# One core, a decoder layer with a 16,384-expert FFN: gathered tokens in groups of 32, finished in steps, and gate tables built by two engines

## The chip, the cores and the metric

The kernel runs on one core of a Trainium2 chip. The core has TensorE (PE, its weight loads shown as PEld), VectorE (DVE), ScalarE (ACT), GpSimd (POOL) and SyncE (SP), whose queue issues most transfers; GpSimd's own queue issues the indirect ones. The metric is the device time of one execution in microseconds, the median of several runs. All arithmetic is float32; large products are taken as three matmuls of a rounded part and a rest (hi and lo).

## The reference, cut to what matters

The layer mixes tokens (RWKV-7 and Mamba-2 heads), and then runs a PEER expert FFN over 512 tokens of width 2048. Only the last part is touched:

```python
def one_block(xb):
    q = (xb @ w_query).reshape(PEER_BLOCK, PEER_HEADS, 2, PEER_HALF)
    s = jnp.einsum('lhpd,hpnd->lhpn', q, sub_keys)
    s_half, i_half = lax.top_k(s, PEER_TOPK)
    ...                                   # 8 heads x 16 experts for each token
    eidx = jnp.take_along_axis(cand_i, pos, axis=-1)
    gates = jax.nn.softmax(top_s, axis=-1)
    u = u_emb[eidx]
    act = gelu(jnp.einsum('ld,lhkd->lhk', xb, u))
    return jnp.einsum('lhk,lhkd->ld', gates * act, v_emb[eidx])
h = h + gate2 * peer_ffn(n, ...)
return rms_norm(h, final_norm_w)
```

Each token so uses 128 of the 16,384 rows of u and of v.

## The kernel before

The FFN treats its tokens in two ways. The first 320 (TD) go **densely** through all experts; the last 192 (TG) have their 128 rows **gathered**.

Dense work comes in units, 128 of each kind. A u unit (`expert_u`) multiplies 128 experts' u rows with 320 tokens: 48 matmuls of 128x320 into `mm`, then a Gelu. Its weights come as four tiles `wr` of 256 KB; ScalarE casts each to `whi`, GpSimd subtracts for `wlo` (line 198). A v unit (`expert_v`) does the same with v rows (`vr`, `vhi`, `vlo`) into four tiles `po` that are added to the stream `hT`. Ahead of each four v units, `expert_g` takes a slice `gd` of the gate table, multiplies the activations by it and splits the product into `ghi` and `glo`.

The gate table says what weight each dense token gives each expert. `gate_block` builds it, ten blocks of 32 tokens: for each token two one-hot tiles of 128x128, J and I2 (I2 holds the gates), are made on VectorE by comparing with `iota`, and one matmul into `pg` multiplies them. ScalarE copies four tokens' result to `gb`, and a transfer of 2 MB writes the block to memory (`glD`), since v units read it in another order. The first v unit needs all ten blocks.

Gathered tokens are fed in between by `pace`, called once for each dense unit: it starts up to two gathers while the count of units allows it, spread over NGU of the 256 units, and at most NGB tiles `g` are held. A slot "u" gathers one row of u for each of 128 (token, slot) pairs, and VectorE takes the dot products with the tokens' rows, in two halves (line 1242). When a group is through, `weights` makes `wT`, the gates times the Gelu of the dot products. A slot "v" gathers one token's 128 rows of v; four tokens' gathers make four parts (`part`), each of which sums 512 columns of four tokens with four matmuls into four quarters of the tile `pw` (line 1258); ScalarE copies it, and a transfer writes `yG`. Parts are taken one at a time between the chunks of a dense unit.

When all slots are done, `gathered` reads `yG` back, turns it, adds it to the stream, takes the norm of all 192 tokens and writes them.

An engine works in the order of its instructions. That order is set by the Tile scheduler, which plays the program through; it is fixed when the kernel is built.

## Time and profile before

| | before |
|---|---|
| median of 3 runs | 4190.32 us (4183.4 to 4191.96) |
| profiled execution, its own time | 4183.04 us |
| its span | 4180.8 us |
| TensorE busy | 3789.5 us (91%) |
| VectorE busy | 2403.2 us (57%) |
| ScalarE busy | 1433.6 us (34%) |
| GpSimd busy | 2475.7 us (59%) |
| TensorE's mean granted clock | 0.941 |
| moved by transfers | 958.67 MB, mean 229 GB/s |

A busy share over the whole span is an average over stages with different limits; what bounds a stage is read from its own stretch. The granted clock is a share of full speed.

### The profile page before, as it was taken

How to read it: one execution, taken by the hardware profiler on the slowest of the kernel's cores; microseconds unless marked ns; L12 is line 12 of the kernel's file. 1: busy time of each engine (PE TensorE's matmuls, PEld its weight loads, DVE VectorE, ACT ScalarE, POOL GpSimd, SP SyncE). 2: the span in 40 equal slices, each digit the busy share in tenths (PEclk: the TensorE clock that was granted, in tenths of full speed). 3: DMA queues.
4: the chain of work that ended last, by engine and by line, in shares of the span. 5: the costliest groups of instructions: out<-in, count | busy, mean ns of one | idle time of the engine just before them, and what ended most of it. 6: DMA issues, size and time to landing. Idle time of an engine off the chain costs nothing. (4 is left out here: it accounts for less than half of the span.)

```text
span 4180.8 us, 65986 instructions
## 1 busy us (share of the span) xinstructions
PE 3789.5 (91%) x23694; PEld 3071.0 (73%) x23694; DVE 2403.2 (57%) x4909; ACT 1433.6 (34%) x2778; POOL 2475.7 (59%) x1919
## 2 busy tenths in 40 slices
PE   5899989999988996888688999999999999999978
PEld 3667656776657995777577877888787777777668
DVE  7442245466614999999867676667765221222234
ACT  3443324433324212222223333333333343433333
POOL 5445433433316434655377777888888776676646
PEclk9999999988969998998799999999999999999979
DMA  8465652333344225777688888897988788788843
GB/s 345 163 201 194 200 141 72 81 114 94 117 138 131 89 71 203 279 293 273 238 322 285 321 292 315 298 338 287 323 315 315 287 295 305 288 297 299 291 134 128
DMA packets 378503, 958.67 MB, mean 229 GB/s; under 512 B 62080, under 2 KB 127488, under 8 KB 322560
## 3 DMA queue, kind: packets, MB, share of 16 engines
q1 hardware_dynamic: 322880, 551.79, 40.1%
q0 software_dynamic: 55296, 402.68, 25.1%
q8 instruction: 186, 3.05, 0.3%
q14 instruction: 141, 1.16, 0.1%
HBM read 908.97 MB, written 45.29 MB: 228 GB/s over the span
## 5 line engine op out<-in xcount | busy, mean ns | idle before, releaser
L198 POOL TENSOR_TENSOR wlo<-wr,whi 128x512 fp32r<-128x512 f32 (+2 forms) x832 | 1119.3, 1357 | 939.0 <-ACT whi L197 829.0
L198 POOL TENSOR_TENSOR vlo<-vr,vhi 128x512 fp32r<-128x512 f32 x512 | 695.1, 1375 | 236.8 <-ACT vhi L197 213.4
L197 ACT CAST whi<-wr 128x512 fp32r<-128x512 f32 (+2 forms) x832 | 505.7, 616 | 908.8 <-PE mm L202 334.0
L203 PE MATMUL mm<-n2hi,wlo 128*128 128x320 f32 x2304 | 736.8, 320 | 27.6 <-POOL wlo L198 27.2
L201 PE MATMUL mm<-n2hi,whi 128*128 128x320 f32 x2304 | 735.3, 320 | 11.6 <-ACT whi L197 9.2
L202 PE MATMUL mm<-n2lo,whi 128*128 128x320 f32 x2304 | 726.3, 315 | 2.4 <-POOL n2lo L198 2.4
L201 PE MATMUL po<-ghi,vhi 128*128 128x320 f32 x2048 | 627.9, 316 | 38.9 <-DVE hT L1207 18.8
L202 PE MATMUL po<-glo,vhi 128*128 128x320 f32 x2048 | 628.6, 313 | 14.0 <-DVE glo L198 14.0
L1242 DVE SCALAR_TENSOR_TENSOR g<-g,row 128x1024 f32<-128x1024 f32 x384 | 616.5, 1645 | 5.4 <-DMA g<-in_u,eix 5.4
L203 PE MATMUL po<-ghi,vlo 128*128 128x320 f32 x2048 | 527.7, 318 | 25.2 <-POOL vlo L198 24.7
L197 ACT CAST vhi<-vr 128x512 fp32r<-128x512 f32 x512 | 311.8, 620 | 596.1 <-PE mm L202 308.0
L203 PEld LDWEIGHTS mm<-n2hi,wlo 128*128 128x128 f32 x2304 | 440.3, 191 | 99.4 <-issue 48.6
L1166 DVE TENSOR_TENSOR act<-gd,act 128x320 f32<-128x320 f32 x128 | 162.5, 1279 | 605.2 <-ACT act L1139 528.0
L201 PEld LDWEIGHTS mm<-n2hi,whi 128*128 128x128 f32 x2304 | 442.0, 192 | 38.5 <-issue 18.5
L202 PEld LDWEIGHTS mm<-n2lo,whi 128*128 128x128 f32 x2304 | 442.0, 192 | 25.1 <-issue 21.8
L201 PEld LDWEIGHTS po<-ghi,vhi 128*128 128x128 f32 x2048 | 389.0, 191 | 89.8 <-issue 28.1
L1207 DVE SCALAR_TENSOR_TENSOR hT<-po,mod,hT 128x320 f32<-128x320 f32 x512 | 248.5, 543 | 324.8 <-PE po L203 311.3
L203 PEld LDWEIGHTS po<-ghi,vlo 128*128 128x128 f32 x2048 | 356.6, 191 | 88.2 <-POOL vlo L198 42.3
L202 PEld LDWEIGHTS po<-glo,vhi 128*128 128x128 f32 x2048 | 390.9, 191 | 31.4 <-issue 15.9
L1258 PE MATMUL pw<-g,wT 128*32 128x512 f32 x1536 | 293.6, 617 | 20.2 <-ACT ys L1261 11.6
L1235 POOL DMA_INDIRECT g<-in_u,eix x192 | 227.7, 1186 | 120.5 <-DVE I L1127 29.2
L201 PE MATMUL mm<-nhi,whi 128*128 128x512 f32 x640 | 261.4, 408 | 4.5 <-ACT whi L197 4.5
(438 smaller groups left out, 5890.3 us busy)
## 6 DMA issues: line engine op xcount, KB each, us to landing
wr<-in_uT SPq DMA_DIRECT2D x512, 256.0 KB
vr<-in_v SPq DMA_DIRECT2D x512, 256.0 KB
wr<-in_wrest SPq DMA_DIRECT2D x160, 256.0 KB
aw<-in_ada SPq DMA_DIRECT2D x32, 1024.0 KB
a2w<-in_adar SPq DMA_DIRECT2D x64, 512.0 KB
glD<-gb SPq DMA_DIRECT2D x10, 2048.0 KB
gd<-glD SPq DMA_DIRECT2D x32, 640.0 KB
a3w<-in_adar SPq DMA_DIRECT2D x32, 512.0 KB
```

Of the source, the lines that this page charges most:

```text
L197: copied.append(S.copy(hi, src))
L198: return (eng or V).tensor_tensor(lo, src, hi.bitcast(F32), OP.subtract)
L201: TE.matmul(ps, lhsT=whi, rhs=xhi, start=first, stop=False)
L202: TE.matmul(ps, lhsT=whi, rhs=xlo, start=False, stop=False)
L203: done_mm[0] = TE.matmul(ps, lhsT=wlo, rhs=xhi, start=False, stop=last)
L1166: V.tensor_tensor(a.rearrange("p (b t) -> p b t", t=TB), gd[:, :, i, :], a.rearrange("p (b t) -> p b t", t=TB), OP.mult)
L1207: V.scalar_tensor_tensor(h, po[d], mod2[:, 48 + k:49 + k], h, OP.mult, OP.add)
L1235: G.indirect_dma_start(out=g, out_offset=None, in_=I[s[0]], in_offset=bass.IndirectOffsetOnAxis(ap=ix, axis=0))
L1242: V.scalar_tensor_tensor(g[:, c], g[:, c], 1.0, n2s[i][:, c], OP.mult, OP.mult, accum_out=wtp[i][:, e, n:n + 1])
L1258: TE.matmul(ps[32 * j:32 * j + 32, :], lhsT=wT[:, t0 + j:t0 + j + 1].to_broadcast([P, 32]), rhs=gs[j][:, cq], start=True, stop=True, tile_ ...
```

## The change

- **Groups.** Gathered tokens form six groups of 32, each token with four rows of partitions; a u slot gathers 32 tokens x 4 experts. Before, there was one group of 128 tokens and one of 64 with two rows each. Indices and gates take a way through memory (`exD`, `gaD`) to get into that shape. `wT` is made by VectorE's transpose of 32x32 blocks.
- **Order of the slots.** The u slots run 38 slots ahead; then u and v alternate. NGU is 222 (was 200), NGB 6 (was 7), NSP 36 (was 30): the number of u units before the first v unit.
- **v rows summed singly.** One token makes one part: four matmuls, one for each 512 columns of its one gather.
- **Finishing in steps.** After each 64 tokens, five steps (`end_steps`) run between dense units in place of `gathered`.
- **Gate tables.** J for four tokens is one TENSOR_TENSOR; of four I2, two are made by VectorE as before and two by two activations of ScalarE.

```diff
-NGU = 200
+NGU = 222
-NGB = 7
+NGB = 6
-NSP = 30
+NSP = 36
...
+    V.tensor_scalar_mul(ngT, gT[:, 0:TD], -1.0)
...
+            J = gx.tile([P, 4, P], F32, name="J", bufs=2)
+            V.tensor_tensor(J, iota.unsqueeze(1).to_broadcast([P, 4, P]),
+                            jT[:, t0:t0 + 4].unsqueeze(2).to_broadcast([P, 4, P]), OP.is_equal)
+            I2 = gx.tile([P, 4, P], F32, name="I2", bufs=2)
             for i in range(4):
-                J = gx.tile([P, P], F32, name="J", bufs=4)
-                I2 = gx.tile([P, P], F32, name="I2", bufs=4)
-                V.tensor_scalar(J, iota, jT[:, t:t + 1], None, OP.is_equal)
-                V.tensor_scalar(I2, iota, iT[:, t:t + 1], gT[:, t:t + 1], OP.is_equal, OP.mult)
+                if i % 2:
+                    V.tensor_scalar(I2[:, i], iota, iT[:, t:t + 1], gT[:, t:t + 1], OP.is_equal, OP.mult)
+                else:
+                    S.activation(I2[:, i], iota, AF.Abs, bias=iT[:, t:t + 1], scale=-1.0)
+                    S.activation(I2[:, i], I2[:, i], AF.Relu, bias=gT[:, t:t + 1], scale=ngT[:, t:t + 1])
...
-    slots = [("u", 1, n) for n in range(64)] + [("v", n) for n in range(4)]
-    for n in range(P):
-        slots += [("u", 0, n)] + [("v", 4 + n // 2)] * (n % 2 and n < 120)
-    slots += [("v", n) for n in range(64, TG)]
+    for n in range(TG + NS + 6):
+        slots += [("u", n // NS, n % NS)] * (n < TG) + [("v", n - NS - 6)] * (n >= NS + 6)
...
+            if late and late[0][0] <= units:
+                late.pop(0)[1]()
...
+                V.transpose(wT[:, 32 * i:32 * i + 32], wts)
...
-        four.append((g, i))
-        if len(four) < 4:
-            return
+        def part():
             ps = pw2.tile([P, T], F32, name="pw")
-            for j in range(4):
-                TE.matmul(ps[32 * j:32 * j + 32, :], lhsT=wT[:, t0 + j:t0 + j + 1].to_broadcast([P, 32]), rhs=gs[j][:, cq],
+            for q in range(4):
+                TE.matmul(ps[32 * q:32 * q + 32, :], lhsT=wT[:, i:i + 1].to_broadcast([P, 32]), rhs=g[:, T * q:T * q + T],
...
+            if i % TF == TF - 1:
+                late.extend((units + 2 + n, f) for n, f in enumerate(end_steps(i // TF)))
...
+        def add(e):
+            ps = pu.tile([P, 8, TF], F32, name="mm", tag="mm")
+            for d in range(8):
+                TE.transpose(ps[:, d, :], o[0:TF, P * k:P * k + P], ident[0:TF, 0:TF])
+            V.tensor_tensor(sq[:, ks], ps, colk(mod2[:, 48 + 8 * e:56 + 8 * e]), OP.mult)
+            V.tensor_tensor(hg[:, ks], hg[:, ks], sq[:, ks], OP.add)
+            S.activation(sq[:, ks], hg[:, ks], AF.Square)
+            V.tensor_tensor(hg[:, ks], hg[:, ks], colk(col("fw", 8 * e, 8)), OP.mult)
+        def norm():
+            V.tensor_reduce(acc, sq.rearrange("p k t -> p t k"), mybir.AxisListType.X, OP.add)
+            TE.matmul(ps[:, 0:TF], lhsT=ones, rhs=acc, start=True, stop=True)
+            G.tensor_tensor(rn, rn, negh[:, 0:1].to_broadcast([P, TF]), OP.pow)
+            V.tensor_tensor(hg[:, ks], hg[:, ks], rn.unsqueeze(1).to_broadcast([P, 8, TF]), OP.mult)
+            nc.sync.dma_start(out.rearrange("k p t -> p k t")[:, :, TD + TF * f:TD + TF * f + TF], hg)
...
+        return [load, lambda: None, lambda: add(0), lambda: add(1), norm]
```

How this stands in the engines' orders, at three places. First the gate stage. On VectorE, before, between two dot products (`g,wtp<-g,row`) of a u slot:

```order
L1242 SCALAR_TENSOR_TENSOR g,wtp_14866<-g,row 128x1024 x2
L1126 TENSOR_SCALAR J<-iota,jT 128x128
L1127 TENSOR_SCALAR I_15092<-iota,iT,gT 128x128
L1126 TENSOR_SCALAR J<-iota,jT 128x128
L1127 TENSOR_SCALAR I_15097<-iota,iT,gT 128x128
L1126 TENSOR_SCALAR J<-iota,jT 128x128
L1127 TENSOR_SCALAR I_15102<-iota,iT,gT 128x128
L1126 TENSOR_SCALAR J<-iota,jT 128x128
L1127 TENSOR_SCALAR I_15107<-iota,iT,gT 128x128
L1242 SCALAR_TENSOR_TENSOR g,wtp_14866<-g,row 128x1024 x2
```

and on VectorE after, in the same stage:

```order
L1254 SCALAR_TENSOR_TENSOR g,wtp<-g,row 128x1024 x2
L1130 TENSOR_TENSOR J<-iota,jT 128x512
L1136 TENSOR_SCALAR I_15177<-iota,iT,gT 128x128 x2
L1130 TENSOR_TENSOR J<-iota,jT 128x512
L1136 TENSOR_SCALAR I_15192<-iota,iT,gT 128x128 x2
L1254 SCALAR_TENSOR_TENSOR g,wtp<-g,row 128x1024 x2
```

Eight instructions for four tokens became three, and twice as many tokens stand between two u slots. On ScalarE after, where only casts, `gb` copies and Gelus stood, the activations of I2 stand among them:

```order
L1142 COPY gb<-pg 128x128x4
L1139 ACTIVATE I_15254<-iota,iT 128x128 x2
L199 CAST whi<-wr 128x512 x2
L1140 ACTIVATE I_15254<-I_15254,gT,ngT 128x128
L1139 ACTIVATE I_15269<-iota,iT 128x128 x2
L1140 ACTIVATE I_15254<-I_15254,gT,ngT 128x128
L199 CAST whi<-wr 128x512
L1140 ACTIVATE I_15269<-I_15269,gT,ngT 128x128 x2
L1152 ACTIVATE act<-mm 128x320
```

A cast of `whi` now stands behind activations that write a buffer which an earlier gate matmul reads.

Second, the parts on TensorE late in the program, before, with the dense matmuls (`po`) around them:

```order
L1258 MATMUL pw<-g,wT 32x512 x3
L201 MATMUL po<-ghi,vhi 128x320
L202 MATMUL po<-glo,vhi 128x320
...
L202 MATMUL po<-glo,vhi 128x320
L1258 MATMUL pw<-g,wT 32x512
L201 MATMUL po<-ghi,vhi 128x320
L202 MATMUL po<-glo,vhi 128x320
...
L1258 MATMUL pw<-g,wT 32x512 x4
```

and after:

```order
L205 MATMUL mm<-n2hi_11455,wlo 128x320
L1268 MATMUL pw<-g,wT 32x512 x4
L203 MATMUL mm<-n2hi_11456,whi 128x320
...
L205 MATMUL po<-ghi,vlo 128x320 x4
L1268 MATMUL pw<-g,wT 32x512 x4
L203 MATMUL po<-ghi,vhi 128x320
```

Before, a first part stands as three matmuls and, 24 dense matmuls on, one; in the whole order the 768 matmuls stand in 262 such pieces. After, they stand in 191, all but a few of them of four.

Third, GpSimd's queue at the first of the three finishing steps, after; `rnf` is the tile whose power is taken, `g` are gathers:

```order
L1247 DMA g<-in_u,eix 128x2048
L200 TENSOR_TENSOR vlo<-vr,vhi 128x512 x3
L1247 DMA g<-in_v,eT 128x2048
L1309 TENSOR_TENSOR rnf<-rnf,negh 128x64
L200 TENSOR_TENSOR wlo<-wr,whi 128x512 x4
L1247 DMA g<-in_u,eix 128x2048
```

The power over 64 columns stands between the splits of two dense units; before, one power over two columns stood in `gathered`.

## Rows read from the trace of the kernel before

**Rows 1.** Busy us and instructions of each engine in seven stretches

```profile
core 0: us, PE busy (x) PEld busy (x) DVE busy (x) ACT busy (x) POOL busy (x), PEclk, DMA share, GB/s
1624.70:2054.50 429.80, 324.97 (x1984) 304.94 (x1984) 408.21 (x875) 119.20 (x223) 231.98 (x172) 0.87 0.77 281
2054.50:2404.50 350.00, 311.52 (x1865) 272.27 (x1866) 246.33 (x335) 107.09 (x197) 257.78 (x199) 0.95 0.86 306
2404.50:3268.20 863.70, 809.64 (x5036) 695.13 (x5036) 582.19 (x674) 292.70 (x536) 722.29 (x536) 0.99 0.87 309
3268.20:3956.20 688.00, 684.51 (x4426) 536.07 (x4424) 169.49 (x221) 272.81 (x482) 482.34 (x408) 1.00 0.81 295
3956.20:4014.60 58.40, 27.30 (x97) 8.58 (x97) 12.02 (x35) 10.94 (x25) 4.87 (x5) 0.55 0.38 136
4014.60:4164.00 149.40, 149.24 (x1010) 148.97 (x1008) 56.73 (x93) 63.15 (x115) 103.61 (x80) 0.99 0.44 143
4164.00:4180.80 16.80, 1.73 (x9) 1.25 (x9) 8.01 (x19) 1.98 (x5) 4.17 (x5) 0.60 0.46 156
```

**Rows 2.** The same stretches, the part sums (tile pw) alone: PE, PEld, ACT

```profile
2054.50:2404.50 350.00, 31.92 (x138) 4.54 (x138) 9.55 (x17) 0.95 0.86 306
2404.50:3268.20 863.70, 96.02 (x427) 13.29 (x427) 31.84 (x55) 0.99 0.87 309
3268.20:3956.20 688.00, 151.50 (x919) 21.64 (x919) 66.82 (x114) 1.00 0.81 295
3956.20:4014.60 58.40, 14.74 (x58) 1.61 (x58) 4.68 (x8) 0.55 0.38 136
```

**Rows 3.** The gate stage, the gate matmuls (tile pg) alone: PE, PEld, ACT

```profile
1624.70:2054.50 429.80, 134.68 (x640) 110.48 (x640) 44.41 (x80) 0.87 0.77 281
```

**Rows 4.** Timeline of TensorE: start us, us, what; a part in pieces

```profile
3401.54 1.05 PE L1258 MATMUL pw<-g,wT 128*32 128x512 f32 x2
...
3406.23 1.06 PE L1258 MATMUL pw<-g,wT 128*32 128x512 f32 x8
```

**Rows 5.** Tiles J, I, oh and glo: ns min/median/max, first and last start

```profile
L1126 DVE TENSOR_SCALAR J<-iota,jT x320: 268/279/5569, 1622.6 to 2040.0; 128x128 f32<-128x128 f32 x160
...
L1127 DVE TENSOR_SCALAR I<-iota,iT,gT x320: 328/340/5610, 1622.9 to 2040.2; 128x128 f32<-128x128 f32 x160
...
L1075 DVE TENSOR_TENSOR oh<-pf,iota x8: 414/418/419, 1612.1 to 1617.2; 128x256 f32<-128x256 f32 x8
...
L198 DVE TENSOR_TENSOR glo<-act,ghi x4: 484/484/486, 2055.1 to 2056.3; 128x320 fp32r<-128x320 f32 x4
```

**Rows 6.** Groups by line on VectorE, 1680 to 2060: busy us, mean ns

```profile
L1127 DVE TENSOR_SCALAR I<-iota,iT,gT 128x128 f32<-128x128 f32 x288 | 145.6, 506 | 0.0
L1242 DVE SCALAR_TENSOR_TENSOR g<-g,row 128x1024 f32<-128x1024 f32 x104 | 136.1, 1343 | 0.0
L1126 DVE TENSOR_SCALAR J<-iota,jT 128x128 f32<-128x128 f32 x288 | 127.0, 441 | 3.8 <-PE pg L1128 3.7
L1242 DVE DVE_READ_ACCUMULATOR g<-g,row 128x1 f32 x104 | 8.4, 81 | 0.0
```

**Rows 7.** Groups by line, 2400 to 3200

```profile
L198 DVE TENSOR_TENSOR glo<-act,ghi 128x320 fp32r<-128x320 f32 x45 | 86.8, 1932 | 20.5 <-ACT ghi L197 19.6 <-issue 0.8
```

**Rows 8.** Tile row on ScalarE

```profile
L299 ACT COPY row<-mps x8: 265/266/277, 45.1 to 142.8; 128x128 f32<-128x128 f32 x8
```

**Rows 9.** Timeline at the end of the gate stage

```profile
1979.69 0.61 PE L1128 MATMUL pg<-I,J 128*128 128x128 f32 x4
...
2042.08 0.32 SPq L1130 DMA_DIRECT2D glD<-gb  x1
...
2053.45 1.70 DVE L1166 TENSOR_TENSOR act<-gd,act 128x320 f32<-128x320 f32 x4 [12.86 <-DMA gd<-glD]
```

**Rows 10.** Groups by line and shape on GpSimd: powers over eight and two columns

```profile
L597 POOL TENSOR_TENSOR rnb<-rnb,negh 128x8 f32<-128x8 f32 x8 | 13.1, 1640 | 10.7 <-DVE rnb L594 10.7
...
L938 POOL TENSOR_TENSOR rn<-rn,negh 128x2 f32<-128x2 f32 x1 | 0.7, 725 | 44.6 <-DVE rn L937 44.6
```

**Rows 11.** Stretches as in rows 1, from 3000 us

```profile
3000.00:3100.00 100.00, 94.58 (x588) 81.99 (x587) 76.41 (x87) 33.26 (x61) 87.70 (x64) 1.00 0.94 341
```

More of the change, by code (lines that the diff above doesn't have):

```diff
@@ L959, in _hybrid @@
     gT = gp.tile([P, T], F32, name="gT")
-    n2D = dp.tile([2, P, D], F32, name="n2D")
+    n2D = dp.tile([TG, D], F32, name="n2D")
     yG = dp.tile([TG, D], F32, name="yG")
-    ggt = [gq.tile([P, n], F32, name=f"ggt{n}") for n in (P, 64)]
-    eix = [gq.tile([P, n], U32, name=f"eix{n}") for n in (P, 64)]
+    exD = dp.tile([TG, P], U32, name="exD")
+    gaD = dp.tile([TG, P], F32, name="gaD")
+    ggt = gq.tile([P, TG // 32, NS], F32, name="ggt")
+    eix = gq.tile([P, TG // 32, NS], U32, name="eix")
     eT = gq.tile([P, TG], U32, name="eT")
@@ L1152, in _hybrid @@
     units = 0
-    done = []
+    late = []
+    ended = [0]
     def expert_g(grp):
-        gd = vp.tile([P, TD // TB, 4, TB], F32, name="gd", bufs=1)
+        gd = vp.tile([P, TD // TB, 4, TB], F32, name="gd", bufs=2)
         nc.sync.dma_start(gd, glD.rearrange("b j i t -> j b i t")[:, :, 4 * grp:4 * grp + 4, :])
@@ L1167, in expert_g @@
                             a.rearrange("p (b t) -> p b t", t=TB), OP.mult)
-            ghi = vp.tile([P, TD], F32R, name="ghi", bufs=5)
-            glo = vp.tile([P, TD], F32R, name="glo", bufs=5)
+            ghi = vp.tile([P, TD], F32R, name="ghi", bufs=8)
+            glo = vp.tile([P, TD], F32R, name="glo", bufs=8)
             split(ghi, glo, a, V)
@@ L1202, in expert_v @@
             if grp == 31:
-                sqs = vp.tile([P, 4, TD], F32, name="gd", bufs=1)
+                sqs = vp.tile([P, 4, TD], F32, name="gd", bufs=2)
             for d in range(4):
@@ L1213, in expert_v @@
             pace(last)
-            if not (slots or begun or parts or done):
-                done.append(True)
-                gathered()
             if nu < min(128, 4 * grp + 8):
@@ L1219, in expert_v @@
                 nu += 1
-    wts = [gq.tile([P, n], F32, name=f"wts{n}") for n in (P, 64)]
-    wtp = [gq.tile([P, 2, n], F32, name=f"wtp{n}") for n in (P, 64)]
+    wts = gq.tile([P, NS], F32, name="wts")
+    wtp = gq.tile([P, 2, NS], F32, name="wtp")
     begun = []
-    four = []
     held = [0]
@@ L1231, in gather @@
             n2s[s[1]] = va.tile([P, D], F32, name="row", bufs=1)
-            nc.sync.dma_start(n2s[s[1]], n2D[s[1]])
+            for q in range(4):
+                nc.sync.dma_start(n2s[s[1]][32 * q:32 * q + 32, :], n2D[32 * s[1]:32 * s[1] + 32, :])
         held[0] += 1
-        ix = eix[s[1]][:, s[2]:s[2] + 1] if s[0] == "u" else eT[:, s[1]:s[1] + 1]
+        ix = eix[:, s[1], s[2]:s[2] + 1] if s[0] == "u" else eT[:, s[1]:s[1] + 1]
         G.indirect_dma_start(out=g, out_offset=None, in_=I[s[0]], in_offset=bass.IndirectOffsetOnAxis(ap=ix, axis=0))
@@ L1254, in part @@
-        def part(q):
-            cq = slice(T * q, T * q + T)
+            if n == NS - 1:
+                V.tensor_tensor(wts, wtp[:, 0], wtp[:, 1], OP.add)
+                S.activation(wts, wts, AF.Gelu)
+                V.tensor_tensor(wts, wts, ggt[:, i, :], OP.mult)
+                V.transpose(wT[:, 32 * i:32 * i + 32], wts)
+            return
+        def part():
             ps = pw2.tile([P, T], F32, name="pw")
-            for j in range(4):
-                TE.matmul(ps[32 * j:32 * j + 32, :], lhsT=wT[:, t0 + j:t0 + j + 1].to_broadcast([P, 32]), rhs=gs[j][:, cq],
-                          start=True, stop=True, tile_position=(0, 32 * j))
-            ys = vp.tile([P, T], F32, name="ys", bufs=2)
+            for q in range(4):
+                TE.matmul(ps[32 * q:32 * q + 32, :], lhsT=wT[:, i:i + 1].to_broadcast([P, 32]), rhs=g[:, T * q:T * q + T],
+                          start=True, stop=True, tile_position=(0, 32 * q))
+            ys = gq.tile([P, T], F32, name="ys", bufs=2)
@@ L1261, in part @@
             S.copy(ys, ps)
-            for j in range(4):
-                nc.sync.dma_start(yG[t0 + j:t0 + j + 1, cq], ys[32 * j:32 * j + 1, :])
-            held[0] -= 4 * (q == 3)
-        parts.extend(lambda q=q: part(q) for q in range(4))
-    def weights(i):
-        w = wts[i]
-        V.tensor_tensor(w, wtp[i][:, 0], wtp[i][:, 1], OP.add)
-        S.activation(w, w, AF.Gelu)
-        V.tensor_tensor(w, w, ggt[i], OP.mult)
-        ps = pw2.tile([P, T], F32, name="pw")
-        if i == 0:
-            TE.transpose(ps[:, 0:P], w, ident)
-            S.copy(wT[:, 64:TG], ps[:, 0:P])
-        else:
-            for hs in (slice(0, 64), slice(64, 128)):
-                TE.matmul(ps[hs, 0:64], lhsT=w[hs, :], rhs=ident[hs, hs], start=True, stop=True)
-            S.copy(wT[:, 0:64], ps[:, 0:64])
@@ L1326, in _hybrid @@
         expert_v(grp)
-    while slots or begun or parts:
+    while slots or begun or parts or late:
         while parts:
@@ L1331, in _hybrid @@
         pace(done_mm[0])
-    if not done:
-        gathered()
     rr = rms_all(pu, "mm", gq, sacc[:, 0:TD])
-    rs = vp.tile([P, TD], F32, name="ghi", bufs=5)
+    rs = vp.tile([P, TD], F32, name="ghi", bufs=8)
     S.copy(rs, rr)
```

86 lines of the change are left out of this document (39 added, 47 removed).

## Prediction

> **What bounds the kernel now.** I read the stretches first, cutting the span where the work changes [rows 1]. The profiled execution took 4183.04 us: a span of 4180.8 and 2.2 around it; the median of the runs shown, 4190.32, is 7.3 above that, and I sum against the profiled execution. Nothing ahead of 1624.7 us stands in another order but for a few small copies, so the sum starts there.
>
> The first stretch (1624.7 to 2054.5) builds the gate tables beside the first dense units. The reader is to see VectorE busy for 408 of its 430 us while TensorE is busy for 325 at a granted clock of 0.87: VectorE bounds it. The four stretches behind it hold the rest of the 254 dense units. Take the part sums [rows 2] and the gate matmuls [rows 3] from TensorE's counts in [rows 1] and divide by 48: 28, 36, 96, 73 and 21 units. The last 21 have nothing beside them: 149.4/21 = 7.11 us each, which I take as TensorE's price of a dense unit. With it, 688 us of the fourth stretch leave 688 - 73 x 7.11 = 169 us for its parts, and TensorE is busy throughout: TensorE bounds it. The second and third stretch run with u and v tokens in flight; there something else costs 0.8 to 1.7 us a unit (below). Between them and the last 21 units lie 58.4 us in which TensorE does 27 us of work at half clock: the gathered tokens are finished in one piece, and TensorE, which works in program order, stands.
>
> **The parts.** A part is four matmuls into four column quarters of one tile. In the trace a stretch of one such matmul (two records) takes 1.05 us, and one of all four (eight records) 1.06 [rows 4]: the four run side by side, and one alone costs as much. Before, the four come from four gathers, and the first part of a batch often stands in pieces, as the order's rows show. Counting such pieces in the whole order gives 262 before and 191 after, when all four matmuls hang on one gather. Along the timeline the second stretch has 28 of the 262, the third 90, the fourth 143, and one run of 29 matmuls lies in the 58 us (58 records [rows 2]). So a piece costs 169/143 = 1.18 us in the fourth stretch, and the change takes 261 - 191 = 70 pieces off: 70 x 1.18 = 83 us, certain where TensorE bounds, less where it waits anyhow.
>
> **The gate stage.** J was four TENSOR_SCALAR per four tokens (median 279 ns), now one TENSOR_TENSOR over 512 columns. TENSOR_TENSOR takes 418 ns for 256 columns and 484 for 320 [rows 5], 1.03 ns a column, so 682 ns for 512, against 4 x 279 = 1116. Half of I2 stays on VectorE. In this stretch I2 took 506 ns and J 441 on average, half a dot product 1343 and its read 81 [rows 6]. After: 80 x 0.682 + 160 x 0.506 + some 49 u slots (38, and half of the rest of 62) x 2 x 1.42 = 55 + 81 + 140 = 276 us, against 408. The upper bound is VectorE held up by GpSimd: glo, a TENSOR_TENSOR of 320 columns, averages 1932 ns in the middle of the span [rows 7], which would make J 3.1 us and the sum 247 + 81 + 140 = 468.
>
> By the rows, then, J gets shorter by 0.43 us a group [rows 5]. A rule of the Trainium skill speaks against this edit: VectorE: DVE Perf Modes, section Why `tensor_tensor` can't do 2×_2P or 4×, says that tensor_tensor keeps to one element a cycle in float32 where tensor_scalar may take two. By that rate alone J's 512 columns would take twice as long as now; the rows hold the slower rate already and still come out shorter, since three of four fixed costs go.
>
> ScalarE gets 320 activations of 128 columns; the nearest row is 266 ns for a copy of that size [rows 8], 85 us in all, beside 119 us that it is busy there now: 204 of some 400 us. That is cover enough if nothing waits in its queue; a rival below is that it does.
>
> TensorE is then next: 34 units (the 28 and six more, by NSP 36 for 30) x 7.11 = 242; 320 gate matmuls between 98 us (four records, two matmuls, in 0.61 us [rows 9]) and 135 (their busy time now, waits among them [rows 3]); ten parts, 12 us. That is 352 to 389 us; with 0.8 us of waiting a unit up to 416. I take **400**, so v starts at 2025, not 2054, with six more units done. At the end of the stage before, the last table goes to memory, comes back and is multiplied: from 2042.1 to 2053.5 with TensorE idle [rows 9]. After, the order has the last gate matmul three units (some 25 us) ahead of the first v unit, which hides these 11 us.
>
> **The paced stretch.** 226 - 6 = 220 units remain: 220 x 7.11 = 1564, and 181 pieces x 1.18 = 214. Waits: the second stretch before has 350 - 36 x 7.11 - 28 x 1.18 = 61 us over (1.7 a unit), the third 864 - 96 x 7.11 - 90 x 1.18 = 75 (0.8 a unit). By the list of slots the third runs two u to one v, and 427/8 = 53 v tokens [rows 2] in 96 units make 0.55 v and 1.1 u a unit. After, 384/222 = 1.73 slots go with each unit, u and v in turn from the 39th on, 0.87 each: less VectorE work a unit than in the third, and GpSimd as busy: there it has 722/96 = 7.5 us a unit [rows 1], four splits and some 1.64 gathers, and here a tenth of a gather more. I take the third's 0.8 for the units with u tokens in flight, from the 36th to the 200th (the last u is slot 346, and 346/1.73 = 200): 164 x 0.8 = 131 us. Bounds: 0 (as in the fourth stretch) and 1.7 (as in the second), so 0 to 279.
>
> **The finishing.** The 58.4 us go. In their place come three times five steps between units. Sixteen transposes each lie on TensorE (48 in all, about 15 us with short waits for their tile). One step is dearer than it looks: GpSimd's pow now runs over 64 columns. Pow took 725 ns for 2 columns and 1640 for 8 [rows 10], 0.15 us a column, so about 10 us for 64. The rows of the order show what stands behind it in GpSimd's queue: four splits of wlo, for which TensorE waits. ScalarE and GpSimd run up to four tiles (one unit) ahead, which covers a part; I take 7 us each, 20 in all, between 0 and 30.
>
> An I2 of 340 ns took up to 5610 [rows 5], so VectorE is at times held for the length of GpSimd's work. The Trainium skill, SBUF — State Buffer, section Who interferes with whom, says that GpSimd and a VectorE operation with two SBUF inputs, or in a two-port mode, exclude each other for the whole instruction. By that rule VectorE would stand for the same 10 us, three times, and the sum would be up to 10 us more where TensorE then waits for glo.
>
> **Sum.** 1624.7 + 400 + 1564 + 214 + 131 + 20 + 15 + 16.8 (the last stretch, unchanged) = 3985.5, and 2.2 around it: **3988**, 195 us less than the profiled execution.
>
> **The rivals.**
> Transfers bind (chance 0.17). A unit moves four tiles of 256 KB and 1.73 gathers of 128 rows of 8 KB (1.049 MB), with the gate slices 2.94 MB. At 7.11 + 0.87 x 1.18 + 0.8 = 8.9 us that is 329 GB/s. The third stretch averaged 309 with queues 0.87 busy; for it speaks that over 300 is rare. Against it, one stretch of 100 us moved 341 at 0.94 [rows 11]. Held to 309, a unit takes 9.5 us: 0.6 x 164 + 0.4 x 26 = 108 us more, 4096.
> The waits nearly vanish (0.13), since u tokens are spread thinner: without 131 and 20 it is 3837; half of it, 3912.
> The tables move the work but don't shorten the stage (0.08), if J is held up as glo is: 468 + 27 us in place of 400, so 4083.
> ScalarE's queue stalls, and the kernel is slower (0.03). The activations of I2 stand ahead of casts of whi, for which splits and dense units wait, and an activation waits until TensorE has read the I2 of two groups ago, which hangs on J. If each of the 80 groups holds the queue for more than 195/80 = 2.4 us, all is lost; at 3 us it is 4228. Against it: in the order an activation has a cast or copy on either side, and ScalarE idles half of that stage.
> No change (0.01) would need the pieces, the stand of 58 us and the stage all to be covered by something unseen.
>
> **How the numbers follow.** The forecast has the remaining 0.58, 3930 to 4040 for its own part. From 3880 to 4100 the range takes in the forecast, the transfers' case, the held J and half of the case without waits; what is left out is the other half, the slower case and tails. About 0.2%, some 8 us, is what a measurement of this kernel can tell from no change. Faster by more: 0.95; within: 0.01; slower: 0.04.
>
> **What would show it.** Right: VectorE below 0.8 busy in the gate stage and v's first matmul near 2025; stretches of eight records wherever parts stand; no stand of TensorE near the end, and 26 units at 7.1 us; three pows of about 10 us. Wrong: a rate that stays at 309 GB/s with queues near 0.9 and units of 9.5 us; wlo as what ends most of TensorE's idle time; whi late by ScalarE in the gate stage.

## The result, and the profile after

The changed kernel took 4037.31 us (median of four runs, 4028.36 to 4060.61) beside 4191.14 for the kernel before on the same chip: a ratio of 0.9645, 95% interval 0.9603 to 0.9688. It is faster, by 154 us. The profiled execution took 4028.36 us, a span of 4026.3. The sum had given a span of 3985.5, so 41 us have to be explained. This execution was the fastest of the four; the median lies 9 us above it.

The page after, the line of busy times and the line of transfers. TensorE is busy 128 us less than before, and 6 MB more are moved:

```profile
PE 3661.0 (91%) x23705; PEld 3044.2 (76%) x23705; DVE 2398.0 (60%) x4504; ACT 1521.6 (38%) x3090; POOL 2547.7 (63%) x1921
...
DMA packets 392370, 964.60 MB, mean 240 GB/s; under 512 B 76080, under 2 KB 141360, under 8 KB 335920
```

The stretches after, cut again where the work changes; they answer to [rows 1]:

```profile
core 0: us, PE busy (x) PEld busy (x) DVE busy (x) ACT busy (x) POOL busy (x), PEclk, DMA share, GB/s
1617.00:2029.00 412.00, 349.07 (x2335) 323.69 (x2333) 329.77 (x443) 242.76 (x574) 277.85 (x198) 0.95 0.88 322
2029.00:2345.70 316.70, 286.50 (x1790) 247.84 (x1791) 218.38 (x305) 104.16 (x195) 243.58 (x184) 0.95 0.91 323
2345.70:2635.00 289.30, 271.85 (x1806) 237.79 (x1805) 189.56 (x215) 104.47 (x193) 252.16 (x189) 0.99 0.94 337
2635.00:2690.00 55.00, 45.67 (x300) 39.82 (x299) 40.86 (x41) 17.53 (x33) 46.66 (x30) 0.91 0.77 286
2690.00:3318.00 628.00, 581.01 (x3770) 506.93 (x3769) 391.11 (x453) 216.15 (x405) 515.49 (x394) 0.97 0.92 328
3318.00:3372.00 54.00, 43.90 (x286) 37.84 (x286) 37.60 (x41) 17.21 (x32) 44.78 (x29) 0.91 0.75 275
3372.00:3580.00 208.00, 192.78 (x1253) 168.28 (x1255) 131.11 (x149) 71.93 (x134) 176.38 (x133) 0.97 0.93 334
3580.00:3800.00 220.00, 220.00 (x1499) 181.15 (x1492) 47.38 (x75) 90.75 (x162) 160.94 (x134) 1.00 0.87 297
3800.00:3860.00 60.00, 53.22 (x352) 52.44 (x352) 23.93 (x31) 21.18 (x38) 46.79 (x29) 0.94 0.49 148
3860.00:4009.00 149.00, 149.00 (x1017) 148.76 (x1015) 49.87 (x80) 63.66 (x117) 106.30 (x83) 1.00 0.41 136
4009.00:4026.30 17.30, 1.76 (x10) 1.24 (x9) 8.20 (x19) 2.17 (x5) 4.18 (x5) 0.63 0.44 152
```

The reader is to see five things. The gate stage ends at 2029 and holds 34 units, counted from 1610.6, where the third dense unit begins (the sum counts from the same unit, 1624.7 in the kernel before). The stretch behind it (2029 to 2346) is 33 v units back to back: TensorE's counts divided by 48, as in the prediction, leave 316.7 - 33 x 7.11 - 26 x 1.18 = 51 us of waiting, 1.6 a unit. Of these TensorE is idle for 30; for the other 21 it is busy longer than its price, at a granted clock of 0.95. The other stretches up to 3580, without the finishings, have 0.9 a unit, with GpSimd busy for 0.82 to 0.87 of the time. The three finishings (55, 54 and 60 us) hold some 38 us more than their units. From 3580 to 4009 TensorE is busy without a gap but for the third finishing, and no stand is left at the end.

One part of the gain is luck. The first Gelu of a dense unit, in the profile before and in the one after:

```profile
L1139 ACT ACTIVATE act<-mm x128: 427/432/444, 1624.2 to 4136.1; 128x320 f32<-128x320 f32 x128
```

```profile
L1152 ACT ACTIVATE act<-mm x128: 415/437/482, 1610.1 to 3981.3; 128x320 f32<-128x320 f32 x128
```

It starts 14 us earlier. In the experiments below, none of which edits anything ahead of it, it starts between 1613.1 and 1630.8. So most of the 14 us are scatter between executions and no work of the change, and a span set beside the 4026.3 holds up to 21 us of it; below, where it matters, times are counted from the first dense unit of each profile.

### The profile page after: what moved, and what is told of

Read it like the earlier page. It is cut to its first block, busy times and chain, and to the rows that moved or that the text cites. A ratio compares the mean times of both kernels' runs of the same rounds, so it can differ in the third digit from the quotient of the medians.

```text
span 4026.3 us, 65357 instructions
## 1 busy us (share of the span) xinstructions
PE 3661.0 (91%) x23705; PEld 3044.2 (76%) x23705; DVE 2398.0 (60%) x4504; ACT 1521.6 (38%) x3090; POOL 2547.7 (63%) x1921
## 5 line engine op out<-in xcount | busy, mean ns | idle before, releaser
L200 POOL TENSOR_TENSOR vlo<-vr,vhi 128x512 fp32r<-128x512 f32 x512 | 710.3, 1408 | 204.7 <-ACT vhi L199 177.9
L1254 DVE SCALAR_TENSOR_TENSOR g<-g,row 128x1024 f32<-128x1024 f32 x384 | 714.8, 1900 | 33.7 <-DMA g<-in_u,eix 33.7
L204 PE MATMUL po<-glo,vhi 128*128 128x320 f32 x2048 | 619.6, 311 | 0.0
L205 PE MATMUL po<-ghi,vlo 128*128 128x320 f32 x2048 | 475.4, 317 | 23.0 <-POOL vlo L200 22.5
L1179 DVE TENSOR_TENSOR act<-gd,act 128x320 f32<-128x320 f32 x128 | 150.6, 1183 | 449.1 <-ACT act L1152 435.3
L205 PEld LDWEIGHTS po<-ghi,vlo 128*128 128x128 f32 x2048 | 342.0, 190 | 80.3 <-POOL vlo L200 59.5
L205 PE MATMUL mm<-nhi,wlo 128*128 128x512 f32 x640 | 261.3, 408 | 0.0
```

The lines of the kernel that those rows point to most:

```text
L200: return (eng or V).tensor_tensor(lo, src, hi.bitcast(F32), OP.subtract)
L204: TE.matmul(ps, lhsT=whi, rhs=xlo, start=False, stop=False)
L205: done_mm[0] = TE.matmul(ps, lhsT=wlo, rhs=xhi, start=False, stop=last)
L1179: V.tensor_tensor(a.rearrange("p (b t) -> p b t", t=TB), gd[:, :, i, :], a.rearrange("p (b t) -> p b t", t=TB), OP.mult)
L1254: V.scalar_tensor_tensor(g[:, c], g[:, c], 1.0, n2s[i][:, c], OP.mult, OP.mult, accum_out=wtp[:, e, n:n + 1])
```

## The experiments

All ratios are against the kernel before; 0.9645 is the changed kernel. "The middle" below is a stretch of 136 dense units from about the 68th to the 204th, found by counting TensorE's dense matmuls; it holds two finishings wherever it is read below. In the changed kernel:

```profile
2331.50:3581.70 1250.20, 1150.91 (x7510) 1004.37 (x7510) 803.17 (x910) 433.55 (x806) 1050.19 (x784) 0.97 0.91 327
```

### e1: the gate tables as before

```diff
-            J = gx.tile([P, 4, P], F32, name="J", bufs=2)
-            V.tensor_tensor(J, iota..., jT[:, t0:t0 + 4]..., OP.is_equal)
-                    S.activation(I2[:, i], iota, AF.Abs, ...); S.activation(I2[:, i], I2[:, i], AF.Relu, ...)
+                V.tensor_scalar(J, iota, jT[:, t:t + 1], None, OP.is_equal)
+                V.tensor_scalar(I2, iota, iT[:, t:t + 1], gT[:, t:t + 1], OP.is_equal, OP.mult)
```

> The changed kernel with the gate tables built as before (all on VectorE, J and I2 token by token), the rest of the change kept; it computes the same. My theory: VectorE then bounds the gate stage again. In the changed kernel's stage (1617 to 2029) VectorE is busy 330 us, 201 of it on the two tables; with 320 J at 441 ns and 320 I2 at 506 ns, as in the stage of the kernel before, the tables take 303 us, so VectorE is busy 432 and the stage takes about 450 instead of 412: 4075 us, between 4060 and 4095. Rival: the splits on GpSimd and ScalarE and the dense matmuls (TensorE is busy 349) set the stage's length by now; then it stays within 10 us, 4030 to 4047.

Measured: 4063.2 us, 0.9721 (0.9696 to 0.9746); span 4062.5. The tables by two engines are worth some 32 to 36 us. VectorE's groups by line in the gate stage (busy us, mean ns, then the idle time ahead), first of e1, then of the changed kernel:

```profile
L1133 DVE TENSOR_SCALAR I<-iota,iT,gT 128x128 f32<-128x128 f32 x316 | 162.1, 513 | 0.0
L1132 DVE TENSOR_SCALAR J<-iota,jT 128x128 f32<-128x128 f32 x316 | 156.8, 496 | 37.6 <-PE pg L1134 37.3
```

```profile
L1136 DVE TENSOR_SCALAR I<-iota,iT,gT 128x128 f32<-128x128 f32 x156 | 122.3, 824 | 0.0
L1130 DVE TENSOR_TENSOR J<-iota,jT 128x512 f32<-128x512 f32 x78 | 78.7, 1009 | 50.2 <-PE pg L1141 50.2
```

319 us of tables became 201. My theory holds: the time lies in its range, and TensorE waits 63 us for I there, where it waited 29 for I and J. Counted from the first dense unit, e1 is 45 us behind at the 36th, 34 at the 68th and 31 at the end. It takes back both the wide J and ScalarE's half of I2, so it doesn't say what each is worth by itself.

### e5: 30 u units ahead instead of 36

```diff
-NSP = 36
+NSP = 30
```

> The changed kernel with 30 u units ahead of the first v unit instead of 36, as before the change; it computes the same. My theory: the gate stage is as long as the tables' chain makes it (VectorE is busy 330 us of 412 and waits another 50 for TensorE to give back the tables), so six units fewer beside it shorten it by little, 412 to some 390, and those six cost 9 us each later: some 30 us slower, 4050 to 4080. Rival: the stage goes with the dense units and shrinks by six of them, 60 us, and the stretch with v units alone, which has 1.5 us of waiting a unit, gets shorter: 4020 to 4037.

Measured: 4033.71 us, 0.9649 (0.9615 to 0.9684); span 4035.2. No difference that the runs can tell. The time lies in the rival's range and not in mine. v began at 1996.3, 33 us earlier (46 counted from the first dense unit), so the stage did shrink with its units, by most of the 60 us that the rival wanted; but the six units cost that much later.

### e2: the finishing's power over one column

```diff
-            TE.matmul(ps[:, 0:TF], lhsT=ones, rhs=acc, start=True, stop=True)
-            G.tensor_tensor(rn, rn, negh[:, 0:1].to_broadcast([P, TF]), OP.pow)
+            TE.matmul(ps[0:TF, 0:1], lhsT=acc, rhs=ones[:, 0:1], start=True, stop=True)
+            G.tensor_tensor(r1[0:TF], r1[0:TF], negh[0:TF, 0:1], OP.pow)
+            TE.transpose(pr[:, 0:TF], r1[0:TF].to_broadcast([TF, P]), ident[0:TF, 0:TF])
```

> The changed kernel, with the finishing's power taken over one column on 64 partitions and spread afterwards by a transpose on TensorE, instead of over 64 columns on 128 partitions; it computes the same. My theory: the three powers of 10.6 us on GpSimd hold back the splits of wlo behind them, and of the 10 to 14 us that each finishing costs some 8 are theirs: 4037 - 3 x 8 = 4013 us, between 4005 and 4022, with TensorE's waits for wlo at the three places gone. Rival: the splits ahead cover the power, and a finishing costs what it costs through its transposes and VectorE's passes: within 6 us of 4037.

Measured: 3994.66 us, 0.9563 (0.9533 to 0.9592); span 3994.1, 32 us below the changed kernel's. That is more than I expected, nearly 11 us for each power. Timeline of the changed kernel at its first power (start us, us, engine, line, what, idle time ahead):

```profile
2661.53 10.59 POOL L1309 TENSOR_TENSOR rnf<-rnf,negh 128x64 f32<-128x64 f32 x1
2672.10 1.25 POOL L200 TENSOR_TENSOR wlo<-wr,whi 128x512 fp32r<-128x512 f32 x1
...
2673.41 0.63 PE L205 MATMUL mm<-n2hi,wlo 128*128 128x320 f32 x1 [7.84 <-POOL wlo L200]
2673.84 0.47 PE L203 MATMUL mm<-n2hi,whi 128*128 128x320 f32 x1
2674.11 0.47 PE L204 MATMUL mm<-n2lo,whi 128*128 128x320 f32 x1
...
2678.64 0.42 PE L203 MATMUL mm<-n2hi,whi 128*128 128x320 f32 x1
2678.89 0.31 PE L204 MATMUL mm<-n2lo,whi 128*128 128x320 f32 x1
```

and its stretches of 5 us there (columns as above):

```profile
2660.00:2665.00 5.00, 4.29 (x36) 2.86 (x34) 4.20 (x12) 2.71 (x5) 4.57 (x2) 1.00 0.98 352
2665.00:2670.00 5.00, 0.57 (x8) 0.00 (x0) 1.18 (x4) 0.59 (x1) 5.00 (x1) 0.86 0.10 39
2670.00:2675.00 5.00, 1.59 (x6) 1.59 (x7) 2.85 (x1) 0.00 (x0) 5.00 (x4) 0.50 0.07 26
2675.00:2680.00 5.00, 5.00 (x24) 5.00 (x23) 5.00 (x5) 1.24 (x2) 4.52 (x4) 0.61 0.30 59
```

TensorE stood 7.84 us for the split behind the power. Then it worked at a granted clock of 0.50 (1.2 GHz), where it had 1.00 (2.4 GHz) before it stood: from 2673.41 to 2678.64 twenty matmuls follow each other every 0.27 us, and at full clock every 0.15. That is 2.4 us more: 10.2 in all. The transfers stood too, at 26 to 59 GB/s. At the second and third power TensorE waited

```profile
PE po L205 <- POOL vlo L200: 7.3, 1, 7.3
PE mm L205 <- POOL wlo L200: 6.8, 1, 6.8
```

and then also worked at 0.50 for 5 to 6 us: 22 us of waits and some 7 of the slower clock for the three. VectorE was not held up by the power, for which the prediction had allowed up to 10 us. Inside the first power it ran two halves of a dot product at the shortest time that they take in this trace (1.207 us; 2.12 on average in the middle):

```profile
2663.81 1.21 DVE L1254 SCALAR_TENSOR_TENSOR g<-g,row 128x1024 f32<-128x1024 f32 x1
2664.95 1.22 DVE L1254 SCALAR_TENSOR_TENSOR g<-g,row 128x1024 f32<-128x1024 f32 x1
```

In e2 the same place, GpSimd's timeline:

```profile
2665.36 0.60 POOL L1309 TENSOR_TENSOR rnf<-rnf,negh 64x1 f32<-64x1 f32 x1
2665.92 5.01 POOL L200 TENSOR_TENSOR wlo<-wr,whi 128x512 fp32r<-128x512 f32 x4
```

### e4: the finishings after the last dense matmul

```diff
-                late.extend((units + 2 + n, f) for n, f in enumerate(end_steps(i // TF)))
+                ends.append(i // TF)
 ...
+    with tc.issue_after(done_mm[0].ins):
+        for f in ends:
+            for step in end_steps(f): step()
```

> The changed kernel with the steps of all three finishings after the last dense matmul instead of between units; it computes the same. My theory: what the finishings cost between the units (38 us, some 30 of it the three powers) comes back at the end as a stand of TensorE, in which GpSimd takes the three powers one after another (32 us) and VectorE's passes add some 15, less than that overlapped with the last norm of 17 us: 5 to 25 us slower than 4037, 4040 to 4062. Rival: between the units the steps also hold up what follows them, and at the end the three overlap well: 10 us faster or more, below 4027.

Measured: 4031.32 us, 0.9631 (0.961 to 0.9651); span 4025.7. No difference that the runs can tell; the time lies below my range and above the rival's. The last addition to hT starts at 3968.0 instead of 4009.5. That is 41.5 us earlier, and 52 counted from the first Gelu of each profile (1620.5 here, 1610.1 there), so the finishings cost some 52 us between the units; and the end, 17.3 us before, became

```profile
3969.00:4025.70 56.70, 8.11 (x47) 6.92 (x47) 28.95 (x46) 4.83 (x9) 36.58 (x8) 0.53 0.27 74
```

some 40 us longer. In e2 the same addition comes 36 us earlier by the same count (3976.7, first Gelu 1613.1), so the 52 fall into 36 for the three powers and 16 for everything else. The stretches of the changed kernel, which leave out what a finishing does to the units beside it, gave 38.

### e3: parts in two pieces

```diff
-            for q in range(4):
+            for q in (2 * h, 2 * h + 1):
 ...
-                    parts.pop(0)()
+                    with tc.issue_after(done_mm[0].ins):
+                        parts.pop(0)()
```

> The changed kernel with each part taken as two pieces of two matmuls, one after the next dense tile; it computes the same. In TensorE's order the matmuls of parts then stand in 254 pieces (125 of two, 125 of four) instead of 191, nearly as many as in the kernel before. My theory, a piece costs 1.18 us however many of the four quarters it has: 63 x 1.18 = 74 us more where TensorE bounds, somewhat less where it waits anyhow: 4085 to 4110 us. Rival: a piece of two costs half a piece of four, or lies in waits that are there in any case: 4030 to 4050.

Measured: 4053.26 us, 0.9705 (0.9673 to 0.9738); span 4051.4, 25 us more. By place: 42 of the 63 additional pieces lie in the middle, and it did not get longer (1248.2 us beside 1250.2); 18 lie in the stretch of v units, which is 15 us longer, 3 in the gate stage, which is 6 longer, and none behind the middle, where TensorE is busy throughout. The first dense unit came 7 us later.

```profile
2353.20:3601.40 1248.20, 1179.30 (x7510) 994.75 (x7508) 781.22 (x913) 435.96 (x804) 1059.31 (x782) 0.99 0.91 327
```

TensorE is busy for 28 us more in the same time. So a piece costs nothing in the middle: there something else sets the pace, and the pieces fall into waits. The 15 us in the stretch of v units are no clear price either, since one wait for ghi, 8.4 us in the changed kernel, is longer by 9.4 here:

```profile
PE po L203 <- ACT ghi L199: 17.8, 1, 17.8
```

The time misses my theory's range by 32 us and the rival's by 3; the rival's second half, waits that are there in any case, is what the middle shows. The price of a piece where TensorE bounds was not tested, as no piece was added there; for it stand the rows of the kernel before alone.

### e7 and e6: half of VectorE's dot products, half of the v rows

```diff
-            for e in range(2):
+            for e in range(1):
```

> The changed kernel with the dot product of a gathered u row taken over its first half only (and counted twice), so half of each u row is left out of the result; the gathers are the same. VectorE loses one operation of 1.4 to 1.9 us for each of 384 slots less half, 192 x 2 tokens: some 1.9 us a slot. My theory: the waits of TensorE with u tokens in flight come from VectorE, which is late with po and with the gates (in 2029 to 2346, 31 of the 51 us). Then that stretch loses 30 to 45 us, the later ones some 0.4 us a unit, together 60 to 110: 3930 to 3980 us, the gate stage at most 20 of it. Rival, transfers bind: 0 to -15 us, since the rate stays. Rival, GpSimd's splits bind: -10 to -30, only by what GpSimd gains when VectorE leaves it alone.

Measured: 3939.02 us, 0.9435 (0.9409 to 0.9461); span 3934.2. The size is what I expected of VectorE as the cause: counted from the first dense unit, the gate stage loses 29 us, the v units 17, the middle 56. But in the middle TensorE hardly waits for VectorE: in the changed kernel for acc, 2.9 us, and for hT not at all. What changed is GpSimd. Its splits there, by line, in the changed kernel and in e7:

```profile
L200 POOL TENSOR_TENSOR vlo<-vr,vhi 128x512 fp32r<-128x512 f32 x275 | 393.1, 1454 | 84.0 <-ACT vhi L199 66.3 <-PE po L205 10.2 <-DMA vr<-in_v 4.5
L200 POOL TENSOR_TENSOR wlo<-wr,whi 128x512 fp32r<-128x512 f32 x271 | 362.4, 1368 | 33.5 <-ACT whi L199 31.2 <-DMA wr<-in_uT 1.0
```

```profile
L200 POOL TENSOR_TENSOR vlo<-vr,vhi 128x512 fp32r<-128x512 f32 x277 | 366.8, 1349 | 95.3 <-ACT vhi L199 74.0 <-DMA vr<-in_v 14.4 <-PE po L205 2.9
L200 POOL TENSOR_TENSOR wlo<-wr,whi 128x512 fp32r<-128x512 f32 x268 | 344.5, 1315 | 41.7 <-ACT whi L199 36.0 <-DMA wr<-in_uT 3.1 <-issue 0.6
```

With its gathers GpSimd is busy 993 us instead of 1050: 57 us less work, 56 us less time, and TensorE's wait for wlo falls from 73.4 to 43.7. So it looks as the last rival had it, GpSimd gaining from what VectorE leaves out, only larger; the run doesn't prove it, since VectorE itself does less too. The Trainium skill, SBUF — State Buffer, section Who interferes with whom, says that a VectorE instruction with two SBUF inputs contends with a GpSimd instruction that reads SBUF; the dot product is one, and the shorter splits agree. The power doesn't: it reads SBUF too, and the two halves inside it ran undelayed (1.21 and 1.22 us, above).

```diff
-        G.indirect_dma_start(out=g, ..., in_=I[s[0]], ...)
+        src, w = (I["u"], D) if s[0] == "u" else (I["v"].rearrange("r (h n) -> (r h) n", h=2), D // 2)
+        G.indirect_dma_start(out=g[:, 0:w], ..., in_=src, ...)
```

> The changed kernel, whose gathers of v fetch only half a row (4 KB instead of 8); the part sums use that half twice, so half of each gathered v row is left out of the result. Instructions on all engines are the same, only 192 gathers move 0.52 MB less each. Rival, transfers bind: between 2029 and 3600 the queues are 0.91 to 0.94 busy at 320 to 340 GB/s, a unit with its gathers moves some 2.9 MB, and 0.46 MB less is 16%, more than the 1.0 us of waiting in 9.1 us a unit; so most of the 165 us of waits go: 3880 to 3930 us. My theory, that the waits come from VectorE and GpSimd being late (draining po, multiplying act by the gates, splitting): next to nothing, 4015 to 4037.

Measured: 3960.92 us, 0.9489 (0.9459 to 0.952); span 3958.9. That lies between the theories. 25 us went in the stretch of v units and 48 in the middle:

```profile
2303.30:3505.70 1202.40, 1149.27 (x7502) 996.76 (x7501) 783.86 (x909) 443.36 (x802) 1062.11 (x783) 0.98 0.84 288
```

There TensorE's wait for wlo fell from 73.4 to 12.7 us, and waits for VectorE's glo and ScalarE's ghi (24 us) came instead. GpSimd hardly changed: it is busy for 1062 us beside 1050, and its gathers stand in the same pairs ahead of splits, 92 in the middle beside 89. So neither GpSimd's load nor the pairs alone make the waits for wlo. But with shorter transfers the scheduler ordered the other engines anew. VectorE's dot products now come early enough to wait for their rows,

```profile
L1255 DVE SCALAR_TENSOR_TENSOR g<-g,row 128x1024 f32<-128x1024 f32 x234 | 445.4, 1936 | 249.2 <-DMA g<-in_u,eix 237.3 <-issue 10.6 <-DMA g<-in_v,eT 1.3
```

where in the changed kernel they never do in the middle, and ScalarE idles 51 us ahead of its copies of parts instead of 203. So this run does not separate bytes from order. That the transfers are no ceiling at 327 GB/s is shown by e7, e10 and e11, which move 342 to 350 in the same stretch.

### e8: the gathers spread

I then looked at one wait of the middle. Timeline of the changed kernel, GpSimd, TensorE and ScalarE:

```profile
2859.43 0.96 POOL L1247 DMA_INDIRECT g<-in_v,eT  x1
2860.69 0.94 POOL L1247 DMA_INDIRECT g<-in_u,eix  x1 [0.30 <-issue]
2861.64 2.52 POOL L200 TENSOR_TENSOR wlo<-wr,whi 128x512 fp32r<-128x512 f32 x2
...
2860.99 0.75 PE L205 MATMUL po<-ghi,vlo 128*128 128x320 f32 x4
2862.97 0.41 PE L205 MATMUL mm<-n2hi,wlo 128*128 128x320 f32 x1 [1.23 <-POOL wlo L200]
...
2857.10 0.61 ACT L199 CAST whi<-wr 128x512 fp32r<-128x512 f32 x1
```

The cast that the first wlo needs was through at 2857.7. Two gathers, begun together at a unit's end, stood ahead of the split, and TensorE waited 1.23 us for it.

```diff
-            for _ in range(2):
+            for _ in range(1 if nu > NSP else 2):
+                begin()
 ...
+                if i in (0, 2):                 # in a v unit, behind its first and third split
+                    with tc.issue_after(last.ins):
+                        begin()
```

> The changed kernel with the gathers spread: after the gate stage one is begun at the end of a unit and the others after the first and the third split of a v unit, instead of up to two together at the end of each unit; it computes the same. In GpSimd's order 66 pairs of gathers stand directly ahead of the four splits of a u unit in the changed kernel; here 24 do, and 89 single ones. My theory now (from the trace of the changed kernel: two gathers of 0.95 us stand ahead of a split of wlo whose input has been there for 1.6 us, and TensorE waits 1.2 us for it): the waits of the paced stretch are GpSimd's pairs. Then most of the 73 us that TensorE waits for wlo between 2331 and 3582 goes, less what GpSimd's own load (0.84 busy there) gives back: 40 to 70 us, 3965 to 3995. Rivals: transfers or VectorE pace the stretch, and the waits come back at another place: 4020 to 4037.

Measured: 3994.62 us, 0.9566 (0.9541 to 0.9591); span 3991.4, 35 us below the changed kernel's; the middle took 42 us less.

```profile
2335.20:3543.30 1208.10, 1134.81 (x7511) 990.61 (x7510) 821.09 (x910) 438.10 (x803) 1075.32 (x782) 0.98 0.93 337
```

The time is at the upper end of my range. The pairs matter, but they are not most of the waits: for wlo TensorE still waits 56.7 us instead of 73.4, for vlo 11.2 instead of 17.8. That is 23 of the 42 us; another 16 are TensorE's own busy time, at a granted clock of 0.98 for 0.97. GpSimd is now busy for 0.89 of the stretch.

### e9: spread gathers and the narrow power

> The power over one column (measured alone: about 36 us less than the changed kernel) and the spread gathers together; it computes the same. If the waits for wlo come from the pairs of gathers and the power's 10 us are paid in full, both gains stand: 3995 less 40 to 65, 3930 to 3955 us. If the two take the same waiting time away: 3960 to 3995.

Measured: 3973.08 us, 0.9517 (0.949 to 0.9543); span 3965.2. The time lies in the second range, but the sum of the gains nearly stands: counted from the first dense unit, 36 and 40 us alone make 69 together. Whether they share the other 7 these runs can't tell.

### e10 and e11: a quarter of the splits taken from GpSimd

e10 leaves the fourth low part out; e11, on top of e9, has VectorE compute it:

```diff
-                last = split(vhi, vlo, vr, G)
+                last = split(vhi, vlo, vr, V if i == 3 and slots else G)
```

> The changed kernel in which GpSimd computes only three of the four low parts of each dense unit while tokens are in flight behind the gate stage; the fourth tile's third products use the low part of the tile before, so these low parts are left out of the result. TensorE, VectorE, ScalarE and the transfers have the same work. My theory, GpSimd paces the stretch with tokens in flight (7.7 us busy of 9.0 a unit, and TensorE waits for its splits): GpSimd falls to some 6.2 us, and TensorE bounds at 7.11 + 0.85 x 1.18 = 8.1 us: 136 units x 0.8 = 110 us less and some 10 in the stretch of v units, 3905 to 3940. Rivals: VectorE (its dot products of 2.1 us) or the transfers (0.91 to 0.94 busy at 330 GB/s, which 8.1 us a unit would have to raise to 360) pace it: at most 30 us less, 4005 to 4037.

Measured: 3956.47 us, 0.9459 (0.9439 to 0.9478); span 3949.5, 77 us less. The middle:

```profile
2329.00:3494.60 1165.60, 1122.57 (x7486) 988.94 (x7486) 615.61 (x900) 437.71 (x801) 838.20 (x642) 0.99 0.95 345
```

With VectorE's and the transfers' work as it was, the middle is 85 us shorter, far more than the rivals allowed: GpSimd's splits have the largest part in its pace that a run shows. VectorE is busy 188 us less too, for the same operations (a half dot product takes 1.64 us there, 2.12 in the changed kernel), so the run alone would not clear it; but TensorE had hardly waited for it. It is not all of the 110 that I expected, and the time misses my range by 16 us; the two powers (22 us) are still in it.

> The power over one column and the spread gathers as in the last run (ratio 0.9517), and beside these VectorE computes the fourth low part of each dense unit while tokens are in flight; it computes the same. If GpSimd paces the stretch and VectorE (0.64 busy there) has room: 1.4 us a unit less on GpSimd against 0.7 to 1.0 more on VectorE, which gives 20 to 60 us, 3915 to 3955. Rival: VectorE works in order and the split stands behind dot products of 2 us and more, so TensorE waits for VectorE instead: within 10 us of 3973, or up to 40 slower.

Measured: 3951.58 us, 0.9438 (0.9422 to 0.9454); span 3951.2. This version beats both kernels: 234 us less than the kernel before, 87 less than the changed one. The time lies in the range for GpSimd as the pace. The middle, 31 us shorter than in e9 (1189.0) though VectorE has these splits to make as well:

```profile
2344.60:3502.90 1158.30, 1126.44 (x7496) 989.83 (x7495) 781.33 (x1050) 435.81 (x798) 852.13 (x643) 0.99 0.96 350
```

1158.3/136 = 8.52 us a unit, where 7.11 + 0.87 x 1.18 = 8.13 is TensorE's own price.

### e12: u units ahead to the end

```diff
-            if nu < min(128, 4 * grp + 8):
+            if nu < min(128, 4 * grp + NSP + 4):
```

> The version of the last call with VectorE's quarter of the splits (ratio 0.9438), and beside it the u units stay some 36 ahead of the v units to the end, so no stretch of v units alone follows the gate stage; it lies at the end instead, when the tokens are through. All 128 outputs of u units then go through memory (36 before), 30 MB more of transfers. It computes the same. My theory: v units back to back with tokens in flight cost 9.4 to 12.6 us each after the gate stage, since TensorE waits for VectorE to drain po and to make the gates' products, and 7.1 at the end, where VectorE is nearly idle; 33 units at 8.5 instead of 10.2 give 40 to 60 us, 3890 to 3915. Rival, transfers pace the stretch (0.94 busy): 30 MB more at 330 GB/s cost up to 90 us, spread over the stretch, and the gain is lost: 3950 to 4000.

Measured: 4131.03 us, 0.9871 (0.9846 to 0.9896); span 4129.2: 178 us slower than e11 and outside both ranges. The rival's direction, but not its reason: the transfers moved 326 to 332 GB/s here, less than in e11. Waits between 2345 and 3400, on TensorE and on VectorE (us in total, times, longest):

```profile
PE po L206 <- ACT ghi L202: 72.2, 15, 11.7
```

```profile
DVE act L1184 <- DMA act<-actD: 139.1, 35, 17.4
```

Each act now comes back from memory; VectorE waits for it, ghi is late, and TensorE stands. Whether other buffers or an earlier load would mend this was not tried, so the run says nothing on the stretch of v units.

## Why the prediction was right, and where it was short

**Right.** TensorE has the prices that it had: 3860 to 4009 is 149/7.11 = 21 units, and 3580 to 3800 is busy throughout. v's first matmul is at 2029.1 for 2025. The parts stand together, 184 of 191 pieces with all four matmuls. The stand of 58 us [rows 1] is gone. The powers took 10.59 us, where 0.15 us a column gave 10. J's median is 682 ns, the sum's price. Transfers did not bind at 309 GB/s, nor did ScalarE hold up whi in the gate stage (under 2 us of waiting).

**Right by luck: when the gate stage ended.** From the third dense unit it took 418 us where the sum had 400. VectorE was busy for 0.80 of the stage, at the mark that was to show the forecast right and not below it. That is 330 us where the sum had 276, since J took 1009 ns on average for 682, and I2 824 for 506. TensorE idled for 63 us, 29 of them for J and I2. VectorE no longer fills the stage, but it still sets part of its length, as half of the dot products gone took 29 us off it (e7). That v began near 2025 all the same is due to the 14 us by which this profile was earlier ahead of the dense units.

**Short: the waits.** The step that failed is "I take the third's 0.8 for the units with u tokens in flight": 131 us, and 165 came. 25 of the 34 lie in the 33 v units behind the gate stage, which waited 1.6 us each. The kernel before has nearly the same sequence, 31 v units and 5 u units, in its second stretch [rows 1], and I had worked 1.7 out of it; I took the third stretch's number since the number of tokens a unit was nearer. The rest comes from the middle, at 0.9.

**Short: the power.** The step "which covers a part; I take 7 us each, 20 in all" had the wait right: 7.8, 7.3 and 6.8 us, 22 in all, of powers of 10.6. What it lacked is TensorE's clock, which was at 0.50 for some 5 us behind each wait and cost 7 more, so that the powers cost 29 us at their places and 36 by taking them away (e2). The transposes and short waits were 16 for 15 (e2, e4). So the finishings came out at 38 by the stretches and 52 by moving them, beside 35.

Gate 18, waits 34, finishing 3 by the stretches: 55 us, of which the earlier start gave 14 back. These are the 41 us.

**The pieces** were in the sum with 83 us, and no run shows that. Where 42 more of them were put in the middle they cost nothing (e3). What the rows do show is where they went: before, 143 stood in the stretch that TensorE bounds; after, 38 stand there (from 3580), the others mostly in the middle. What the new order of the slots, which moved them, is worth by itself was not tested, and neither were the buffers that the kernel also got with the change: two for gd instead of one, eight for ghi and glo instead of five.

**What paces the middle** I had seen in VectorE's load ("less VectorE work a unit than in the third, and GpSimd as busy"). 91 of the 99 us that TensorE idles there are waits for wlo and vlo, which GpSimd makes; taking a quarter of its splits away gave 85 us (e10), spreading its gathers 42 (e8). That VectorE matters through GpSimd (e7) is likely and not shown. And GpSimd is not alone: e6 left its load and its pairs of gathers as they were and still took 48 us off. Whether there the bytes did it or the orders of ScalarE and VectorE, which the scheduler changed with it, stays open; e8, e10 and e11 changed those orders too. That wlo would end most of TensorE's idle time I had named as a sign against the forecast; it ended about half, 97 of the 199 us from 1617 to 4009, and 73 of the 99 in the middle.

**Open.** Of the v units behind the gate stage, which took 325 us for 32 units, e8, e10 and e11 changed little (322 to 333), e7 took 17 off and e6 25. TensorE's waits there are

```profile
PE po L203 <- DVE hT L1222: 23.4, 17, 6.2
PE po L203 <- ACT ghi L199: 8.4, 1, 8.4
```

so VectorE's late draining of po is the likeliest cause, but why half the v bytes help more than half the dot products is not settled.

## What to carry to other kernels

Price the waits of a stretch by a row with the same sequence of work, not by one with the same mean load. An operation given to an in-order engine that feeds TensorE can cost nearly its full length even where a part of it is covered, if TensorE's clock falls behind the wait, as with the powers here: make it narrow, or put it where nothing queues behind. And try spreading what such an engine issues: it gave 40 us here, about half of it in waits for the splits behind the gathers. Before calling a busy engine the one that sets the pace, look for a run that leaves its work alone and is faster all the same.
